# Hybrid decoder step on one core: meta tokens' values and weights in zero-filled tiles of their own, and the first tokens normalised in another order

## Chip, cores and metric

The kernel runs on one core of a Trainium2 chip. The metric is the device time of one execution in microseconds, as the median of several executions. Engines are called as the profile calls them: PE (matrix products), PEld (its weight loads), DVE, ACT, POOL and SP; a queue of an engine that issues transfers has a q behind its name (ACTq).

## The reference, cut to what matters

One layer over 16 learned meta tokens, 512 prompt tokens and 8 sample tokens, in float32. All tokens are normalised, and one projection gives the queries, keys and values of both groups of heads; eight heads are a linear recurrence (HGRN2), eight are differential attention. The weights of an attention head are the difference of two softmaxes, and keys 0 to 15 of every query are the meta tokens.

```python
def project(h, norm_g, w_in, lb):
    z = rmsnorm(h, norm_g) @ w_in
    hq, hf, hi, hg, aq, ak, av, ag = jnp.split(z, SPLIT_OFFSETS, axis=-1)
    ...

def diff_attend(q, k, v, q_pos, k_pos, rel_bias, lam):
    ...
    s = jnp.where(dist >= 0, s + bias, NEG_INF)
    p = jax.nn.softmax(s, axis=-1)
    w = p[:, 0] - lam * p[:, 1]
    return jnp.einsum('bhqk,bkhv->bqhv', w, v.astype(jnp.float32))
```

The sample tokens attend to 2048 cached keys each, which lie in pages, with a bias that is one value for all pages but the last and another for the last page.

## The kernel before, in words

All work stands in one program whose order on each engine is the order in which the Python code emits it; lines 1393 to 1399 bind it. Nearly every instruction is recorded through one helper, so the profile shows line 168 for it, and the tiles tell what it is.

The projection runs block by block (64 blocks of 128 columns for the inputs, 16 for the outputs). A block has four groups of 128x512 weights. `split` makes a high part (`hi`, on ACT) and a low part (`lo`, on DVE) of a group's weights, and `group` multiplies them on PE with the high and low parts of the tokens (`xh`, `xl`), 12 products for each half of the tokens. The first half is prompt tokens 0 to 255 (tiles 0 and 1), the second is tiles 2 and 3 with the meta and sample tokens.

Lines 439 to 483 are an order written out by hand, in which block 0 is multiplied while the prompt tokens are made. For tile j, `norm_stat(j)` takes squares with their sum and a reciprocal root on ACT (one chain of four instructions), `norm_scale(j, q)` scales a quarter on DVE, and `to_columns(j, g)` transposes a quarter on PE, copies it out of PSUM to `xh` on ACT and takes the difference to `xl` on DVE. Two halves of the PSUM space take the transposes in turn, two buffers each. Block 0 is multiplied in its halves by `group(u, xh, xl, z)`.

From then on the main loop issues one group after another, and after each of them lets a list of Python generators go on by one step: the attention of prompt heads (`attn`, four steps to a head, pipelined over steps n to n+4), the recurrence (`hgrn`), the softmax of sample tokens (`softmax_dec`), and products with cached values (`value_step`, PE, tile `t_pv`). A planner with its own clock (`fill`) decides where the DVE's work on cached keys stands.

For each value head, `attn_head` first calls `to_tok`: five transposes on PE into two PSUM buffers of the pool `tp` (which has two), the 24 meta and sample rows first; then two copies on ACT into one tile `vtok` (two buffers, shared with the head two before), and three stores on ACT's queue. In `attn`, a step transposes the weights of one 128-query block into `t_w` and those of the 16 meta keys into columns beside them, or, for the fourth block, into a buffer `t_w2` of its own, which the trace lists as t_w too. ACT copies them to `wT` and to `wmT` (16 rows). Every second step, the output `o` is the sum of products `vtok` by `wT`, and last of the product of the 16 meta rows, `vtok[0:NM, 4, :]` by `wmT`. So there are 16 meta products, two to a head: the first of a head adds to blocks 0 and 1, the second to blocks 2 and 3. The second one stands in the same step in which the tokens of a later head are transposed (lines 933 to 948).

Of the kernel before, what the change touches and what calls it, by code (L numbers as in the profile page):

```python
# [18 lines left out]
P = 128  # L19
# [3 lines left out]
NS = 8  # L23
# [186 lines left out]
def layer_kernel(ctx: ExitStack, tc: tile.TileContext, A):  # L210
# [40 lines left out]
    def tp(name):  # L251
        return clock.tile(pst.tile([P, 512], F32, name=name, tag="tp"), "tp", 2)
# [131 lines left out]
    def norm_scale(j, q):  # L384
        cs = slice(q * 512, (q + 1) * 512)
        V.scalar_tensor_tensor(xs[j][:, cs], xs[j][:, cs], stats[j], gB[:, cs], op0=ALU.mult, op1=ALU.mult)
# [51 lines left out]

    to_columns(0, 0)
    split(0)  # L440
    split(1)
    norm_scale(1, 1)
    to_columns(1, 0)
    to_columns(0, 1)
    norm_scale(1, 2)
    split(2)
    to_columns(1, 1)
    to_columns(0, 2)
    norm_scale(1, 3)
    norm_stat(2)  # L450
    to_columns(1, 2)
    to_columns(0, 3)
    to_columns(1, 3)
    group(0, xh, xl, 0)
    small_columns(0)
    small_columns(1)
    split(3)
    norm_scale(2, 0)
    norm_scale(2, 1)
    group(1, xh, xl, 0)  # L460
    norm_stat(3)
    small_columns(2)
    small_columns(3)
    to_columns(2, 0)
    norm_scale(2, 2)
    norm_scale(2, 3)
    to_columns(2, 1)
    group(2, xh, xl, 0)
    norm_scale(3, 0)
    to_columns(2, 2)  # L470
    norm_scale(3, 1)
    group(3, xh, xl, 0)
    to_columns(2, 3)
    norm_scale(3, 2)
    to_columns(3, 0)
    norm_scale(3, 3)
    to_columns(3, 1)
    group(0, xh, xl, 1)
    to_columns(3, 2)
    group(1, xh, xl, 1)  # L480
    to_columns(3, 3)
# [26 lines left out]
    lb = cp.tile([P, H], F32, name="lb")  # L508
    lb1 = cp.tile([P, H], F32, name="lb1")
    bm = cp.tile([P, 3, H], F32, name="bm")  # L510
    bdec = cp.tile([P, NPG, 2 * H], F32, name="bdec")
    b_far, b_near, b_new = bm[:, 0, :], bm[:, 1, :], bm[:, 2, :]
    rowd = dr.tile([H, W], F32, name="rowd")
    skew = dr.tile([H, P * W], F32, name="skew")
# [5 lines left out]
    def small_constants():  # L520
# [32 lines left out]
            T.matmul(t[:, i * H:(i + 1) * H], oh[:, OF + i * P:OF + (i + 1) * P], relb, start=True, stop=True)  # L553
        V.tensor_copy(bm.rearrange("p m h -> p (m h)"), t[:, :3 * H])
        for c in range(2):
            bv = bdec.rearrange("p g (h c) -> p g h c", c=2)[:, :, :, c]
            V.tensor_copy(bv[:, 0:NPG - 1, :], b_far.unsqueeze(1).to_broadcast([P, NPG - 1, H]))
            V.tensor_copy(bv[:, NPG - 1, :], b_near)
        for h in range(H):
            yield  # L560
            store(out=skew[h].rearrange("(p w) -> p w", w=W), in_=rowd[h:h + 1, :].to_broadcast([P, W]))
# [17 lines left out]
    gSa = cp.tile([P, H, NS], F32, name="gSa")  # L579
    amask = [cp.tile([P, P], F32, name=f"am{i}") for i in range(2)]  # L580
    ktail = [cp.tile([P, 2 * NM], F32, name=f"kt{i}") for i in range(2)]
    for a in amask + ktail:
        G.memset(a, 0.0)


# [211 lines left out]
    def softmax_dec(s):  # L797
        sco = scs[s]
        scp = sco[:, 0:NPG, :]
        V.tensor_tensor(scp, scp, bdec, op=ALU.add)  # L800
        V.tensor_copy(sco[:, NPG, :], snew[:, s].rearrange("p h c -> p (h c)"))
        mx = sm.tile([P, 2 * H], F32, name="mx", bufs=1)
        V.tensor_reduce(mx, sco.rearrange("p g a -> p a g"), axis=AX.X, op=ALU.max)
# [72 lines left out]
    def to_tok(src, h, name, tag, dst, dst_s):  # L876

        t2 = tp("t2_" + name)
        T.transpose(t2[:NM + NS, 0:P], src[:, NKEY:CT], ident)
        t = tp("t_" + name)  # L880
        for j in range(4):
            T.transpose(t[:, j * P:(j + 1) * P], src[:, NM + j * P:NM + (j + 1) * P], ident)
        tok = hw.tile([P, 5, P], F32, name=name, tag=tag, bufs=2)
        S.copy(tok[:NM + NS, 4, :], t2[:NM + NS, 0:P])
        S.copy(tok[:, 0:4, :].rearrange("p j d -> p (j d)"), t)
        store(out=dst[0, 0, NM:NKEY, h, :].rearrange("(j p) d -> p j d", p=P), in_=tok[:, 0:4, :])
        store(out=dst[0, 0, 0:NM, h, :], in_=tok[0:NM, 4, :])
        store(out=dst_s[0, :, 0, h, :], in_=tok[NM:NM + NS, 4, :])
        return tok

    def k_out(h):
        to_tok(ak[h], h, "ktok", "t5", A["k_prompt"], A["k_sample"])
# [20 lines left out]
    def attn_head(h):  # L913
        av = avs[h]
        strip = hw.tile([P, 528], F32, name="strip", tag="t1", bufs=2)
        flat = skew[h]
        clock.arrive(strip, 0.25)
        load(out=strip, in_=bass.AP(tensor=flat.tensor, offset=flat.offset, ap=[[W - 1, P], [1, 528]]))
        vtok = to_tok(av, h, "vtok", "t5", A["v_prompt"], A["v_sample"])
        G.tensor_copy(avS[:, :, h], av[:, T0:CT])  # L920
        for c in range(2):
            cs = slice(c * 64, (c + 1) * 64)
            G.tensor_copy(ktail[h % 2][cs, c * NM:(c + 1) * NM], ak[h][cs, SEQ:NKEY])
        heads[h] = dict(h=h, strip=strip, vtok=vtok, nm=sm.tile([P, 3, 4], F32, name="nm"),
                        s1=sm.tile([P, 4, 2], F32, name="s1"))
        flag(f"head{h}")
        yield
# [3 lines left out]
    def attn():  # L931
        live = {}
        for n in range(4 * H + 4):
            h, j = divmod(n, 4)
            if n < 4 * H and j == 0:
                if f"head{h}" not in flags or flags[f"head{h}"] >= slot[0]:
                    yield f"head{h}"
                head = heads[h]
            i4, i3, i2, i1 = (live.get(n - d) for d in (4, 3, 2, 1))
            if i4:  # L940
                a, jj = i4["head"], i4["j"]
                if jj % 2:
                    o = psv.tile([P, 512], F32, name="o", tag="pv")
                    for i in range(jj):
                        T.matmul(o[:, :2 * P], a["vtok"][:, i, :], a["wT"][:, (2 * i + 1) * P:(2 * i + 3) * P], start=i == 0, stop=False)
                    T.matmul(o[:, P:2 * P], a["vtok"][:, jj, :], a["wT"][:, 0:P], start=False, stop=False)
                    T.matmul(o[:, :2 * P], a["vtok"][0:NM, 4, :], a["wmT"], start=False, stop=True)
                    S.copy(aq[:, a["h"], (jj - 1) * P:(jj + 1) * P], o[:, :2 * P])
                if jj == 3:
                    flag(f"attn{a['h']}")  # L950
                    spawn(norm_chain(aq[:, a["h"], 0:SEQ], SEQ, gat, "ra"), f"attn{a['h']}")
                del live[n - 4]
            if i3:
                a, jj = i3["head"], i3["j"]

                L2, odd = (jj + 1) * P, jj % 2
                t = tp("t_w")
                for i in range(jj + 1):
                    x = NM + (i - odd) % (jj + 1) * P
                    T.transpose(t[:, i * P:(i + 1) * P], i3["p"][0][:, x:x + P], ident)  # L960
                t2, c2 = (t, L2) if jj < 3 else (tp("t_w2"), 0)
                T.transpose(t2[:NM, c2:c2 + P], i3["p"][0][:, 0:NM], ident)
                if not odd:
                    a["wT"] = hw.tile([P, 7 * P], F32, name="wT", tag="t4", bufs=1)
                    a["wmT"] = sm.tile([NM, 2 * P], F32, name="wmT", tag="wmT", bufs=1)
                w2 = a["wT"].rearrange("p (c q) -> p c q", q=P)
                S.copy(w2[:, 0:2 * jj + 1:2] if odd else w2[:, 1:2 * jj + 2:2], t[:, :L2].rearrange("p (c q) -> p c q", q=P))
                S.copy(a["wmT"][:, odd * P:(odd + 1) * P], t2[:NM, c2:c2 + P])
            if i1:
                a, L1 = i1["head"], (i1["j"] + 1) * P + NM  # L970
                for c in range(2):
# [47 lines left out]
    def hgrn(h):  # L1019
# [23 lines left out]
        vt = tp("t_hvt")  # L1043
        for j in range(4):
            T.transpose(vt[:, j * P:(j + 1) * P], v[:, NM + j * P:NM + (j + 1) * P], ident)
        hv8 = sm.tile([NS, P], F32, name="hv8", tag="wmT", bufs=1)
        S.copy(hv8, t[:NS, 0:P])
        store(out=hvd[h], in_=hv8)
        vkm = sm.tile([NM, 2, P], F32, name="vkm", bufs=1)
# [376 lines left out]
```

## Time and profile before

| | us |
|---|---|
| median of 3 executions | 1240.04 |
| lowest, highest | 1238.72, 1245.06 |
| profiled execution, device time | 1245.11 |
| span of the profiled execution, first to last instruction | 1243.3 |

Busy time and share are of the profiled execution. It is longer than the median, so the sum that is made on it is set against both. [...]

### The profile page before, as it was taken

The numbers are of one execution on the slowest core, as the hardware profiler recorded it, in microseconds if no ns is written. First come the engines' busy times: TensorE is split into PE (matmuls) and PEld (weight loads), VectorE is DVE, ScalarE is ACT, GpSimd is POOL, SyncE is SP. The second block draws the span as 40 slices with busy tenths as digits, with TensorE's granted clock in tenths as the row PEclk, the third lists the DMA queues.
The fourth block names the chain that finished last, engine by engine and source line by source line (L and its number), as shares of the span: only waits on it lengthen the run. The fifth ranks groups of instructions, "written<-read, shape, count | busy, mean of one in ns | idle before, by whom it ended". The sixth has DMA issues, their size and how long they took to land.

```text
span 1243.3 us, 24937 instructions
## 1 busy us (share of the span) xinstructions
PE 1207.9 (97%) x9352; PEld 1094.5 (88%) x9352; DVE 897.7 (72%) x1678; ACT 532.6 (43%) x1255; POOL 143.2 (12%) x151
## 2 busy tenths in 40 slices
PE   8999999999999999999999999999999999999995
PEld 6899999986677677888888889999999999999995
DVE  7522498878888888878897886989988956345253
ACT  6322333344545564445355465565422235323223
POOL 2000000100000000012010120122123310022020
PEclk9999999999999999999999999999999999999998
DMA  7353788836666669888888976757978837432223
GB/s 232 98 161 93 238 280 289 287 119 220 223 224 207 187 215 305 287 279 267 290 276 289 324 242 204 240 169 243 268 215 247 257 99 238 115 91 86 86 69 138
DMA packets 240958, 261.03 MB, mean 210 GB/s; under 512 B 8783, under 2 KB 198962, under 8 KB 240171
## 3 DMA queue, kind: packets, MB, share of 16 engines
q1 hardware_dynamic: 57298, 164.09, 38.3%
q10 hardware_dynamic: 183538, 95.34, 27.0%
q8 instruction: 74, 1.21, 0.4%
q14 instruction: 48, 0.39, 0.1%
HBM read 245.94 MB, written 16.14 MB: 211 GB/s over the span
## 4 chain that ended last, share of the span: by engine, by line
PE 79%; DVE 10%; DMA 4%; ACT 3%; issue 2%; ACTq 1%; SPq 0%; DVEq 0%
PE ps L168 65%; PE t_pv L168 4%; DVE qb L168 2%; DVE pgt L168 2%; DVE scd L168 2%; PE o L168 1%; PE ho L168 1%; DVE lo L168 1%; DMA raw<-in_w_out 1%; PE sc L168 1%; DMA raw<-in_w_in 1%; PE up L168 1%; PE t_w L168 1%; PE at L168 1%; DVE p L168 1%
## 5 line engine op out<-in xcount | busy, mean ns | idle before, releaser
L168 PE MATMUL ps<-xh,hi 128*128 128x264 f32 (+2 forms) x2048 | 539.8, 294 | 1.2 <-ACT ak L168 0.8
L168 PE MATMUL ps<-xl,hi 128*128 128x264 f32 (+2 forms) x2048 | 522.5, 286 | 1.1 <-DVE xl L168 1.1
L168 PEld LDWEIGHTS ps<-xh,hi 128*128 128x128 f32 x2048 | 387.5, 189 | 51.6 <-issue 41.7
L168 DVE TENSOR_TENSOR lo<-raw,hi 128x512 fp32r<-128x512 f32 x321 | 253.5, 795 | 216.5 <-ACT hi L168 215.6
L168 PEld LDWEIGHTS ps<-xl,hi 128*128 128x128 f32 x2048 | 388.0, 189 | 2.8 <-issue 2.7
L168 PE MATMUL ps<-xh,lo 128*128 128x264 f32 (+2 forms) x2048 | 333.1, 285 | 0.0
L168 ACT CAST hi<-raw 128x512 fp32r<-128x512 f32 x321 | 196.2, 617 | 242.9 <-PE ps L168 196.0
L168 PEld LDWEIGHTS ps<-xh,lo 128*128 128x128 f32 x2048 | 283.9, 189 | 0.0
L168 DVE TENSOR_TENSOR pgt<-pgt,qb 128x1024 f32<-128x1024 f32 x128 | 156.3, 1221 | 11.7 <-DMA pgt<-in_cache_k 7.0
L168 DVE TENSOR_REDUCE scd<-pgt 128x16 f32<-128x1024 f32 x128 | 155.6, 1216 | 1.7
L168 PE MATMUL ps<-mh,hi 128*128 128x256 f32 (+1 forms) x512 | 129.9, 286 | 0.2 <-ACT y L168 0.2
L168 PE MATMUL ps<-ml,hi 128*128 128x256 f32 (+1 forms) x512 | 128.5, 283 | 0.0
L168 DVE SCALAR_TENSOR_TENSOR qb<-pgt,wd,qb 128x128 f32<-128x128 f32 x360 | 106.8, 371 | 0.0
L168 PEld LDWEIGHTS ps<-mh,hi 128*128 128x128 f32 x512 | 96.5, 188 | 0.7 <-ACT y L168 0.4
L168 PEld LDWEIGHTS ps<-ml,hi 128*128 128x128 f32 x512 | 96.6, 189 | 0.0
L168 PE MATMUL ps<-mh,lo 128*128 128x256 f32 (+1 forms) x512 | 82.4, 283 | 0.0
L168 PEld LDWEIGHTS ps<-mh,lo 128*128 128x128 f32 x512 | 70.3, 189 | 0.0
L168 PE MATMUL t_pv<-pgt,wd 128*32 128x512 f32 x320 | 48.2, 648 | 8.5 <-ACT wmT L168 4.6
L168 POOL TENSOR_TENSOR sd<-sd,vb 128x1024 f32<-128x1024 f32 x8 | 19.4, 2430 | 174.5 <-ACT vb L168 174.5
L168 ACT COPY hgm<-ho 128x128 f32<-128x128 f32 x32 | 8.5, 265 | 70.0 <-PE ho L168 69.9
L168 ACT ACTIVATE p<-p,nm 128x144 f32<-128x144 f32 (+3 forms) x64 | 36.1, 565 | 2.0 <-DVE nm L168 2.0
L168 DVE TENSOR_TENSOR xr<-xr,t_y 128x512 f32<-128x512 f32 (+1 forms) x17 | 11.2, 657 | 31.2 <-PE t_y L168 31.2
(242 smaller groups left out, 1156.0 us busy)
## 6 DMA issues: line engine op xcount, KB each, us to landing
pgt<-in_cache_k SPq DMA_DIRECT2D x128, 512.0 KB
pgt<-in_cache_v SPq DMA_DIRECT2D x128, 512.0 KB
raw<-in_w_in ACTq DMA_DIRECT2D x125, 512.0 KB
raw<-in_w_out ACTq DMA_DIRECT2D x32, 512.0 KB
x<-in_x_prompt SPq DMA_DIRECT2D x4, 1024.0 KB
qb<-qd SPq DMA_DIRECT2D x8, 512.0 KB
sd<-in_state_hgrn SPq DMA_DIRECT2D x8, 512.0 KB
vb<-hvd SPq DMA_DIRECT2D x8, 512.0 KB
```

Of the source, the lines that this page charges most:

```text
L168: r = f(*a, **k)
```

## The change

The order of lines 439 to 481 is another: the squares of tiles 2 and 3 are earlier, the splits of the weights later, and the groups of block 0 stand earlier between the transposes. Then the meta rows get a tile of their own, `few` (one buffer, which `hgrn` uses for its 8 sample rows too); `vmeta` (two) and `wmeta` (one) are 128-row tiles that are zeroed once, and the meta rows are copied to their first 16 rows, so that the meta product has 128 rows. `t_w2` comes from the pool `psv` instead of `tp`. The bias of the cached keys is kept once instead of for each page, and is added in two instructions instead of one.

```diff
     to_columns(0, 0)
     split(0)
-    split(1)
     norm_scale(1, 1)
     to_columns(1, 0)
+    norm_stat(2)
     to_columns(0, 1)
     norm_scale(1, 2)
-    split(2)
+    split(1)
     to_columns(1, 1)
+    group(0, xh, xl, 0)
     to_columns(0, 2)
     norm_scale(1, 3)
-    norm_stat(2)
+    split(2)
+    norm_stat(3)
     to_columns(1, 2)
+    group(1, xh, xl, 0)
+    norm_scale(2, 0)
     to_columns(0, 3)
     to_columns(1, 3)
-    group(0, xh, xl, 0)
     small_columns(0)
     small_columns(1)
     split(3)
-    norm_scale(2, 0)
+    to_columns(2, 0)
+    group(2, xh, xl, 0)
     norm_scale(2, 1)
-    group(1, xh, xl, 0)
-    norm_stat(3)
+    norm_scale(3, 0)
     small_columns(2)
     small_columns(3)
-    to_columns(2, 0)
+    to_columns(2, 1)
     norm_scale(2, 2)
+    to_columns(3, 0)
+    group(3, xh, xl, 0)
+    norm_scale(3, 1)
     norm_scale(2, 3)
-    to_columns(2, 1)
-    group(2, xh, xl, 0)
-    norm_scale(3, 0)
     to_columns(2, 2)
-    norm_scale(3, 1)
-    group(3, xh, xl, 0)
+    to_columns(3, 1)
+    norm_scale(3, 2)
+    group(0, xh, xl, 1)
     to_columns(2, 3)
-    norm_scale(3, 2)
-    to_columns(3, 0)
     norm_scale(3, 3)
-    to_columns(3, 1)
-    group(0, xh, xl, 1)
     to_columns(3, 2)
     group(1, xh, xl, 1)
     to_columns(3, 3)
...
-    bdec = cp.tile([P, NPG, 2 * H], F32, name="bdec")
+    bdec = cp.tile([P, 2, 2 * H], F32, name="bdec")
...
-            bv = bdec.rearrange("p g (h c) -> p g h c", c=2)[:, :, :, c]
-            V.tensor_copy(bv[:, 0:NPG - 1, :], b_far.unsqueeze(1).to_broadcast([P, NPG - 1, H]))
-            V.tensor_copy(bv[:, NPG - 1, :], b_near)
+            V.tensor_copy(bdec.rearrange("p g (h c) -> p g h c", c=2)[:, :, :, c], bm[:, 0:2, :])
...
-    for a in amask + ktail:
+    vmeta = [cp.tile([P, P], F32, name=f"vm{i}") for i in range(2)]
+    wmeta = cp.tile([P, 2 * P], F32, name="wmeta")
+    for a in amask + ktail + vmeta + [wmeta]:
         G.memset(a, 0.0)
...
-        V.tensor_tensor(scp, scp, bdec, op=ALU.add)
+        V.tensor_tensor(sco[:, 0:NPG - 1, :], sco[:, 0:NPG - 1, :], bdec[:, 0, :].unsqueeze(1).to_broadcast([P, NPG - 1, 2 * H]), op=ALU.add)
+        V.tensor_tensor(sco[:, NPG - 1, :], sco[:, NPG - 1, :], bdec[:, 1, :], op=ALU.add)
...
-        tok = hw.tile([P, 5, P], F32, name=name, tag=tag, bufs=2)
-        S.copy(tok[:NM + NS, 4, :], t2[:NM + NS, 0:P])
-        S.copy(tok[:, 0:4, :].rearrange("p j d -> p (j d)"), t)
+        tok = hw.tile([P, 4, P], F32, name=name, tag=tag, bufs=2)
+        few = sm.tile([NM + NS, P], F32, name="few", tag="few", bufs=1)
+        S.copy(few, t2[:NM + NS, 0:P])
+        S.copy(tok.rearrange("p j d -> p (j d)"), t)
...
+                S.copy(vmeta[h % 2][0:NM, :], head["few"][0:NM, :])
...
-                    T.matmul(o[:, :2 * P], a["vtok"][0:NM, 4, :], a["wmT"], start=False, stop=True)
+                    T.matmul(o[:, :2 * P], vmeta[a["h"] % 2], wmeta, start=False, stop=True)
...
-                t2, c2 = (t, L2) if jj < 3 else (tp("t_w2"), 0)
+                t2, c2 = (t, L2) if jj < 3 else (psv.tile([P, 512], F32, name="t_w2", tag="pv"), 0)
...
-                    a["wmT"] = sm.tile([NM, 2 * P], F32, name="wmT", tag="wmT", bufs=1)
...
-                S.copy(a["wmT"][:, odd * P:(odd + 1) * P], t2[:NM, c2:c2 + P])
+                S.copy(wmeta[0:NM, odd * P:(odd + 1) * P], t2[:NM, c2:c2 + P])
...
-        hv8 = sm.tile([NS, P], F32, name="hv8", tag="wmT", bufs=1)
+        hv8 = sm.tile([NS, P], F32, name="few", tag="few", bufs=1)
```

## Rows read from the trace of the kernel before

**Rows 1.** Busy time by engine, from the page: us, share of the span, instructions.
```profile
PE 1207.9 (97%) x9352; PEld 1094.5 (88%) x9352; DVE 897.7 (72%) x1678; ACT 532.6 (43%) x1255; POOL 143.2 (12%) x151
```

**Rows 2.** List of waits of PE: us in total, times, longest us.
```profile
PE t_pv L168 <- ACT wmT L168: 4.6, 6, 0.9
PE t_w L168 <- ACT vtok L168: 2.1, 6, 0.3
PE t_sum L168 <- ACT wT L168: 1.1, 1, 1.1
```

**Rows 3.** Timeline of the first 42 us: start, length, engine, operation.
```profile
14.46 1.97 PE L168 MATMUL t_x<-ident,x 128*128 128x128 f32 x8 [1.34 <-DVE x L168]
20.21 1.92 ACT L168 ACTIVATE junk<-x 128x2048 bf16<-128x2048 f32 x1
22.69 1.54 ACT L168 CAST xh<-t_x 128x512 fp32r<-128x512 f32 x3
23.29 1.89 DVE L168 TENSOR_TENSOR xl<-t_x,xh 128x512 fp32r<-128x512 f32 x3 [1.18 <-ACT xh L168]
31.21 1.03 PE L168 MATMUL t_x<-ident,x 128*128 128x128 f32 x8
34.56 0.36 PE L168 MATMUL ps<-xl,hi 128*128 128x264 f32 x1 [1.14 <-DVE xl L168]
35.50 0.65 PE L168 MATMUL ps<-xh,lo 128*128 128x264 f32 x4
41.39 0.28 PE L168 MATMUL ps<-xh,hi 128*128 128x256 f32 x1
```

**Rows 4.** Timeline around meta products: weight loads of PEld, then products of PE.
```profile
279.51 0.19 PEld L168 LDWEIGHTS o<-wT,vtok 128*128 128x128 f32 x1
279.94 0.19 PEld L168 LDWEIGHTS o<-wT,vtok 128*128 128x128 f32 x1
279.29 1.68 PE L168 MATMUL o<-wT,vtok 128*128 128x256 f32 x8
267.78 0.69 PE L168 MATMUL o<-wmT,vtok 16*128 16x256 f32 x2
268.41 0.33 PE L168 MATMUL t_w<-ident,p 128*128 128x128 f32 x1
```

**Rows 5.** Timeline of one head's second meta product and what follows.
```profile
280.90 0.69 PE L168 MATMUL o<-wmT,vtok 16*128 16x256 f32 x2
281.63 0.73 ACT L168 COPY vtok<-t_vtok 24x128 f32<-24x128 f32 x2 [6.02 <-PE o L168]
281.94 0.44 PE L168 MATMUL t_w<-ident,p 128*128 128x128 f32 x2 [0.34 <-ACT vtok L168]
284.26 0.25 ACT L168 COPY wmT<-t_w 16x128 f32<-16x128 f32 x1
284.56 1.08 PE L168 MATMUL t_pv<-pgt,wd 128*32 128x512 f32 x4 [0.78 <-ACT wmT L168]
```

**Rows 6.** Table by stretch: us, busy of PE, PEld, DVE, ACT, POOL, PEclk, DMA share, GB/s.
```profile
284.32:287.72 3.40, 3.16 (x13) 1.50 (x14) 3.26 (x12) 1.93 (x7) 0.00 (x0) 0.50 1.02 312
311.60:315.00 3.40, 2.66 (x21) 1.72 (x21) 2.99 (x10) 2.74 (x9) 0.00 (x0) 1.00 0.82 243
```

**Rows 7.** Timeline: second meta products of the next heads.
```profile
308.83 0.48 PE L168 MATMUL o<-wmT,vtok 16*128 16x256 f32 x1
335.14 0.48 PE L168 MATMUL o<-wmT,vtok 16*128 16x256 f32 x1
```

**Rows 8.** Timeline of ACT around key heads; chain: start, us, what.
```profile
194.12 0.42 ACTq L888 DMA_DIRECT2D out_k_sample<-ktok  x1
204.51 0.25 ACT L168 COPY ktok<-t_ktok 24x128 f32<-24x128 f32 x1 [2.12 <-PE t_ktok L168]
134.51 13.46 DMA raw<-in_w_in
```

**Rows 9.** Groups of DVE by line: count, busy us, mean ns, idle before.
```profile
L168 DVE TENSOR_TENSOR wnew<-scd 128x8 f32<-128x8 f32 x8 | 1.3, 159 | 0.0
```

More of the change, by code (lines that the diff above doesn't have):

```diff
@@ L882, in to_tok @@
             T.transpose(t[:, j * P:(j + 1) * P], src[:, NM + j * P:NM + (j + 1) * P], ident)
-        tok = hw.tile([P, 5, P], F32, name=name, tag=tag, bufs=2)
-        S.copy(tok[:NM + NS, 4, :], t2[:NM + NS, 0:P])
-        S.copy(tok[:, 0:4, :].rearrange("p j d -> p (j d)"), t)
[L886 to L889, printed above, removed]
+        tok = hw.tile([P, 4, P], F32, name=name, tag=tag, bufs=2)
+        few = sm.tile([NM + NS, P], F32, name="few", tag="few", bufs=1)
+        S.copy(few, t2[:NM + NS, 0:P])
+        S.copy(tok.rearrange("p j d -> p (j d)"), t)
+        store(out=dst[0, 0, NM:NKEY, h, :].rearrange("(j p) d -> p j d", p=P), in_=tok)
+        store(out=dst[0, 0, 0:NM, h, :], in_=few[0:NM, :])
+        store(out=dst_s[0, :, 0, h, :], in_=few[NM:NM + NS, :])
+        return tok, few
     def k_out(h):
@@ L918, in attn_head @@
         load(out=strip, in_=bass.AP(tensor=flat.tensor, offset=flat.offset, ap=[[W - 1, P], [1, 528]]))
-        vtok = to_tok(av, h, "vtok", "t5", A["v_prompt"], A["v_sample"])
+        vtok, few = to_tok(av, h, "vtok", "t5", A["v_prompt"], A["v_sample"])
         G.tensor_copy(avS[:, :, h], av[:, T0:CT])
@@ L923, in attn_head @@
             G.tensor_copy(ktail[h % 2][cs, c * NM:(c + 1) * NM], ak[h][cs, SEQ:NKEY])
-        heads[h] = dict(h=h, strip=strip, vtok=vtok, nm=sm.tile([P, 3, 4], F32, name="nm"),
+        heads[h] = dict(h=h, strip=strip, vtok=vtok, few=few, nm=sm.tile([P, 3, 4], F32, name="nm"),
                         s1=sm.tile([P, 4, 2], F32, name="s1"))
```

## Prediction

> **What bounds the kernel now.** I read the busy times first: PE is busy for 97% of the span, and no other engine for more than 72% [rows 1]. So a microsecond counts where PE loses it, and elsewhere only if PE comes to wait. The list of PE's waits is short [rows 2]: what it names of attention sums to 7.8 us, all waits for copies on ACT. Then I read the timeline of the first 42 us, where PE is not yet the bound: the squares of a token tile take ACT 2.48 us (start 20.21, next copy 22.69), the differences on DVE wait 1.18 us for the copies behind them, and PE waits 1.14 us for such a difference before the second half of block 0. Block 1 begins at 41.39 [rows 3]. Last I read the attention steps: the meta products [rows 4], the step in which a head's second meta product stands [rows 5], the granted clock [rows 6] and the spacing of heads [rows 7].
>
> The sum is made on the profiled execution, device time 1245.1 (span 1243.3). The median of the runs is 1240.0, 5.1 less; the term of the clock says why, as I read it.
>
> **First part: the order of the first tokens.** Nothing is added or removed; it is a question of who waits. I laid the old order end to end over PE, ACT and DVE, each step behind the one before it on its engine and behind what it reads, with lengths from the rows: a copy to `xh` holds ACT 0.5 us (three in 1.54), a squares chain 2.48; a scaling or a difference holds DVE 0.6 to 0.7 (three differences in 1.89); four transposes hold PE 0.5, and twice that before about 21.5 us, where eight take 1.97 instead of 1.03. Four products take 0.65 with an end of 0.28, so they follow each other at 0.12, and the twelve of a group and half block hold PE 1.4 us, or 2.6 at half pace [rows 3]. The laid-out end of block 0 is 41.5, against 41.39 in the row; so the laying-out is good to some tenths. The new order laid out in the same way ends at 42.7: 1.2 us later. Why: the squares of tile 2 now stand on ACT directly behind the copy of tile 1's first quarter, at 16.1, and five transposed quarters queue behind them; the next copy goes out at 18.6, DVE dries up for 1.65 us, since the two splits that gave it work there have been moved behind. The first group on PE now comes at 18.0, where PE is at half pace, and holds the next transposes for 2.6 us (DVE dry 0.6). The squares of tile 3, at 22.7, dry it for 1.6 again. In the old order the two chains cost DVE 1.4 and 0.8. At the end the new order has more left to do on PE beside DVE's last differences, which doesn't make up for it. If PE went to full pace some 3 us sooner, which its busier queue may bring, the new order would end level with the old, or 0.4 ahead. Tile 2 must have landed by 16.1; its squares at 20.21 show no wait, so no row says how much sooner they can start, at worst 4 us of ACT. With the split behind them, a load of weights on ACT's queue goes out later too, but its weights are first read in block 1. Term: +1.2, bounds -0.4 and +4.
>
> **Second part: the meta product with 128 rows.** Passes of 128 rows and 256 columns follow each other at 0.215 us (weight loads at 279.51 and 279.94, two passes apart). The two passes of a 16-row product take 0.63 until the next instruction can go (267.78 to 268.41), 0.20 more than two of 0.215. It also begins late: six passes of 256 and two of 128 columns (0.109 each, by the transposes at 31.21) would take 1.51 from 279.29, and the product begins 1.61 after it [rows 4]. So PE loses 0.10 + 0.20 = 0.3 us at each of 16 products, and a product that uses all rows like its neighbours should lose none of it. At the eight first products of a head nothing waits behind: 8 x 0.29 = -2.3 us. [...] The loss that the rows show lies between the passes, and I go by them.
>
> Eight second products of a head: in six of them a copy into the token tile on ACT waits until `o` is done (idle 6.02 before it), and only then frees the buffer for PE's `t_w`, which waits 0.34; after three stores on ACT's queue the copy of `wmT` comes at 284.26, and `t_pv` waits 0.78 for it [rows 5]. In the new kernel the 24 rows go to `few`, which doesn't share the token tile's buffers: its copy is done early and `t_w` doesn't wait. The 512-column copy still waits for `o`, so the ACT queue behind it moves up only by what `o` gains (0.20) and by the copy that went ahead of it (0.73 for both, less some 0.6 for the larger): 0.33 us, and with `t_pv` behind that queue this is what PE gains, 6 x 0.33 = -2.0, bounds -3.8 (the 0.34 and the 0.3 in full) and 0. What remains late there is ACT's queue with its three stores. Two more heads have no tokens behind them: 2 x 0.29 = -0.6.
>
> `t_w2` in another pool: one wait of 1.1 us for `wT` hits a small product (`t_sum`) which took the buffer of `t_w` in turn after `t_w2` [rows 2]; without `t_w2` it takes the other: -1.1, bounds -1.1 and 0.
>
> **Clock.** Four stretches of 3.4 us between 284 and 424 us have a granted clock of 0.50, that is 1.2 GHz, such as that from 284.32; a like step of another head, at 311.60, kept 1.00 [rows 6]. Each follows a step as in [rows 5], in which PE did a 16-row product and small transposes, and waited. The price: from one head's second meta product to the next are 27.93 us with such a stretch (280.90 [rows 5] to 308.83) and 26.31 without (308.83 to 335.14) [rows 7], so 1.6, which is also half of the 3.16 that PE is busy in it [rows 6]. Since the new step has full rows in the place of the 16 and less waiting, I expect all four to go: -6.4, bounds -6.4 and 0. The runs of before lie between 1238.7 and 1245.1, 6.4 apart, as far as four such stretches, so I read the profiled execution as one with four and the median as one with none or one.
>
> **Small things.** Eight copies of 16 rows to `vmeta`, 0.25 each as for `wmT` [rows 5], stand on ACT at a step where PE waits for none of its copies: 0; with that cover gone 2. Eight more additions on DVE, at most 0.16 each as the small ones of `wnew` [rows 9], lie beside PE's work: 0, at most +1.3. The bias copies, the zeroing on POOL and the `psv` buffer, which was free a step before, are 0.
>
> **The sum.** 1245.1 + 1.2 - 2.3 - 2.0 - 0.6 - 1.1 - 6.4 = 1233.9. On the median, where I take the stretches at half clock as mostly not there, 1240.0 + 1.2 - 6.0 = 1235.2. I forecast between them, 1234.5. That is 0.45% below the median; about 0.5%, 6.2 us, is what a measurement of this kernel can tell from no change, so the edge, 1233.8, lies right beside it.
>
> **Rivals.** The half clock stays, or moves to other steps: the step keeps its wait behind ACT's queue, and the start shifts all steps against the stretches. Against it: the product is the largest of the weak work there. A run with four of them gives 1233.9 + 6.4 = 1240.3. Chance 0.12.
>
> Rows don't matter (the padding does nothing): the products stay at 0.63, only the waits go; 1245.1 + 1.2 - 6.4 - 1.1 and 6 x 0.13 less makes 1238.0. Against it the pace in [rows 4]. [...] Chance 0.08.
>
> The start gains instead: if the squares on ACT come where DVE has work, the dry 3.8 us that I count there aren't lost, and the start ends some 3 us before mine: 1231.5. For it: my laying-out hangs on when PE's clock rises and on tenths in the queues. Chance 0.22.
>
> Slower: `few` has one buffer where the token tile had two, so a head's copy waits until the stores of the head before have left. Between the last store of one key head and the copy of the next lie 10.39 us (194.12 to 204.51). One load on the same queue took 13.46 us [rows 8]; if stores did, ACT would stand 3 us at each of eight key heads and the splits and PE behind it: 1234.5 + 24 = 1258. It decides from a landing time of 10.4 us on; against it, in the old kernel that load is the only one of this length in the chain. Chance 0.07.
>
> **How the numbers follow.** Forecast 0.51, rivals 0.12, 0.08, 0.22, 0.07. Range 1230 to 1240.3: it takes in the sooner start, the products without gain and the bounds of the small terms and a run with the half clock, and leaves out the stalled copies and what lies beyond two bounds at once. Faster by over 0.5%: the start's case and not quite half of the forecast, 0.44; slower 0.07; within 0.5% the rest, 0.49.
>
> **What would show it.** Block 1 should begin near 42.6, with DVE idle before two differences behind squares. Two passes of the meta product should stand 0.215 apart, and `t_w` follow without a wait for ACT, while `t_pv` still waits for the copy of the weights. Heads should be 26 us apart or less, with no stretch at 0.50. A start that ends before 41, waits of ACT's copies into `few`, or half-clock stretches at other heads would each prove a step wrong.

## The result and the profile after

| | before | after |
|---|---|---|
| median, us | 1239.18 | 1227.51 |
| lowest, highest | 1238.07, 1245.06 | 1225.88, 1229.28 |
| executions | 6 | 6 |
| profiled execution, device time | 1245.11 | 1226.96 |
| its span | 1243.3 | 1225.1 |
| ratio after to before, 95% interval | | 0.990 [0.9886, 0.9914] |

The kernel became 11.7 us faster, twice what was forecast (5.5), and the time lies 2.5 us below the forecast's range. PE's busy time fell from 1207.9 [rows 1] to 1195.9.

The list of PE's waits after (us in total, times, longest), which answers to [rows 2]. `t_w` for `vtok` and `t_sum` for `wT` are gone; `t_pv` still waits for the copy of the meta weights in six steps, 4.4 us in all where it waited 4.6.

```profile
PE t_pv L168 <- ACT wmeta L168: 4.4, 6, 0.8
PE t_x L168 <- DVE x L168: 4.2, 5, 1.6
PE t_x L168 <- issue: 2.3, 1, 2.3
PE t_pv L168 <- DVE st L168: 0.6, 1, 0.6
PE t_vtok L168 <- ACT few L168: 0.3, 1, 0.3
```

The timeline of the start after, for [rows 3] (in brackets the idle time before an instruction, and what ended it). Both squares chains leave DVE waiting 1.51 us for a copy, PE stands idle for 2.27 us in front of the transposes at 27.33, and block 1 begins at 42.70 instead of 41.39.

```profile
16.22 1.91 ACT L168 ACTIVATE junk<-x 128x2048 bf16<-128x2048 f32 x1
18.00 0.56 PE L168 MATMUL ps<-xh,hi 128*128 128x256 f32 x1
19.29 0.69 DVE L168 TENSOR_TENSOR xl<-t_x,xh 128x512 fp32r<-128x512 f32 x1 [1.51 <-ACT xh L168]
...
25.88 0.69 DVE L168 TENSOR_TENSOR xl<-t_x,xh 128x512 fp32r<-128x512 f32 x1 [1.51 <-ACT xh L168]
27.33 0.63 PE L168 MATMUL t_x<-ident,x 128*128 128x128 f32 x4 [2.27 <-issue]
...
42.70 0.28 PE L168 MATMUL ps<-xh,hi 128*128 128x256 f32 x1
```

A first meta product after, for [rows 4]: the last product with `wT` before it, the load of its weights, itself, and what follows. The next instruction goes 0.43 us after it begins (268.75 to 269.18), where it took 0.63.

```profile
268.52 0.38 PE L168 MATMUL o<-wT,vtok 128*128 128x128 f32 x2
268.64 0.30 PEld L168 LDWEIGHTS o<-wmeta,vm 128*128 128x128 f32 x2
268.75 0.60 PE L168 MATMUL o<-wmeta,vm 128*128 128x256 f32 x2
269.18 0.60 PE L168 MATMUL t_w<-ident,p 128*128 128x128 f32 x4
```

A step with a second meta product after, for [rows 5], another head of the same pattern. The 512-column copy starts at 307.25, 0.2 us after the meta product *begins*; before, both copies started when that product had ended (281.63, with the product from 280.90 to 281.59 [rows 5]). The three stores on ACTq (1.3 us) stand, as before, ahead of the copies `aq`, `wT`, `wmeta`.

```profile
307.05 0.60 PE L168 MATMUL o<-wmeta,vm 128*128 128x256 f32 x2
307.25 0.59 ACT L168 COPY vtok<-t_vtok 128x512 f32<-128x512 f32 x1 [1.70 <-PE o L168]
307.49 0.38 PE L168 MATMUL t_w<-ident,p 128*128 128x128 f32 x2
307.87 0.42 ACTq L888 DMA_DIRECT2D out_v_prompt<-vtok  x1
308.33 0.51 ACTq L889 DMA_DIRECT2D out_v_prompt<-few  x1
308.89 0.34 ACTq L890 DMA_DIRECT2D out_v_sample<-few  x1
309.69 0.25 ACT L168 COPY wmeta<-t_w 16x128 f32<-16x128 f32 x1
309.99 1.06 PE L168 MATMUL t_pv<-pgt,wd 128*32 128x512 f32 x8 [0.73 <-ACT wmeta L168]
```

The stretch of [rows 6] after, in the same table: the granted clock stays at 1.00, and between 43 us and PE's last product no stretch at half clock is left. (PEclk is the granted clock of PE as a share of the full one. Here and below half clock is a granted clock of 0.50, and what comes after PE's last product is left out.)

```profile
284.32:287.72 3.40, 3.05 (x24) 2.21 (x25) 3.22 (x12) 2.24 (x8) 0.00 (x0) 1.00 0.99 295
```

Where the 18.2 us between the two spans lie, by the starts of the blocks' first products in the two traces. A second step is the step with a head's second meta product; it is measured from the first product of the group ahead of it to the first product of the group behind it.

| part | predicted | found |
|---|---|---|
| start of block 1 | +1.2 | +1.3 |
| eight first meta products (0.33 each) | -2.3 | -2.7 |
| six second steps (0.75 each where no clock fell) | -2.0 | -4.5 |
| two heads without tokens behind | -0.6 | -0.5 |
| `t_sum` (in block 24) | -1.1 | -1.2 |
| four stretches at half clock | -6.4 | -6.2 |
| blocks 27 to 32, other slots for `t_pv` | 0 | -4.6 |
| blocks 33 to 42, where part of that comes back | 0 | +2.1 |
| all other blocks | 0 | -1.8 |

The first five are found between the same products in both traces. The half clock is what is left of blocks 18 to 26 (227.5 us before, 212.35 after) when the four parts that lie there are taken off. The rows sum to 18.2 within rounding. Of the last row, 1.1 us lies in block 49, which is shorter by as much in the traces of all twelve experiments too, so it belongs to this one execution of the kernel before and not to the change.

The +2.1 is in part work that has moved. A step of `value_step` is eight `t_pv` products; block 27 has two such steps before and one after, and block 41 has none before and one after:

```profile
715.29 1.36 PE L168 MATMUL t_pv<-pgt,wd 128*32 128x512 f32 x8
```

So blocks 27 to 42 together gain 2.5 us (272.0 to 269.5), and not 4.6.

### The profile page after: what moved, and what is told of

It is laid out like the page before. It is cut to its first block, busy times and chain, and to the rows that moved or that the text cites. A ratio compares the mean times of both kernels' runs of the same rounds, so it can differ in the third digit from the quotient of the medians.

```text
span 1225.1 us, 24954 instructions
## 1 busy us (share of the span) xinstructions
PE 1195.9 (98%) x9352; PEld 1092.5 (89%) x9352; DVE 899.0 (73%) x1684; ACT 534.8 (44%) x1263; POOL 142.1 (12%) x154
## 4 chain that ended last, share of the span: by engine, by line
PE 85%; DVE 7%; ACT 3%; DMA 3%; issue 1%; ACTq 0%; SPq 0%; DVEq 0%
PE ps L168 70%; PE t_pv L168 4%; PE ho L168 2%; DVE qb L168 1%; DMA raw<-in_w_out 1%; PE o L168 1%; PE sc L168 1%; DVE scd L168 1%; DMA raw<-in_w_in 1%; PE up L168 1%; DVE pgt L168 1%; PE t_w L168 1%; DVE lo L168 1%; PE at L168 1%; ACT junk L168 1%
## 5 line engine op out<-in xcount | busy, mean ns | idle before, releaser
L168 DVE TENSOR_TENSOR lo<-raw,hi 128x512 fp32r<-128x512 f32 x321 | 256.6, 804 | 211.4 <-ACT hi L168 210.9
L168 PE MATMUL t_pv<-pgt,wd 128*32 128x512 f32 x320 | 45.4, 604 | 5.8 <-ACT wmeta L168 4.4
L168 DVE TENSOR_TENSOR xr<-xr,t_y 128x512 f32<-128x512 f32 (+1 forms) x17 | 11.2, 656 | 31.2 <-PE t_y L168 31.2
```

What stands on the lines that cost most here:

```text
L168: r = f(*a, **k)
```

## The experiments

Each kernel was timed beside runs of the kernel before on the same chip; their medians are 1240.6 (first four), 1242.3 (next four) and 1241.4 (last four), and 1239.2 for the changed kernel. So medians of different groups compare to 2 or 3 us, and where less matters the traces decide, of which there is one for each kernel. The 0.33, 0.77 and the like below are differences between the same products of a block in two traces.

**1. The start's order alone**, put into the kernel before (lines 439 to 483 as after).

```diff
-    split(1)
     norm_scale(1, 1)
     to_columns(1, 0)
+    norm_stat(2)
     to_columns(0, 1)
     norm_scale(1, 2)
-    split(2)
+    split(1)
     to_columns(1, 1)
+    group(0, xh, xl, 0)
...
```

> The kernel before with only the new order of the startup (lines 439 to 483); the meta tokens' weights and products stay as they were. Theory A (the new order costs the start what the records of the changed kernel show: block 1 begins at 42.70 us there and at 41.39 us before): the start gets 1.3 us longer and nothing else moves, so 1239.2 + 1.3 = 1240.5 us, and block 1 begins at 42.7 us. Theory B (the new order is what gives the gain, by another way than through the start: another clock or another placement of later work): 1236 us or less.

Median 1243.07, ratio 1.0017 [0.9998, 1.0036]: no gain, so B falls. The profiled execution begins block 1 at 42.52, as A says; 1.3 us can't be told from 0 by these times, which are spread from 1239.2 to 1249.8; the profiled execution alone has 13.7 us at half clock in three places, the longest (6.8 us) in block 27, where PE waits 2.8 us for `st`.

**2. The old order in the changed kernel**, the same edit the other way round.

```diff
+    split(1)
     norm_scale(1, 1)
     to_columns(1, 0)
-    norm_stat(2)
...
```

> The changed kernel with the old order of the startup put back; only the meta tokens' part of the change is left. Theory A (the start order costs 1.3 us and the meta tokens' part gives all of the gain): 1227.5 - 1.3 = 1226.2 us, block 1 begins at 41.4 us. Theory B (the start order carries part of the gain): 1228.5 us or more.

Median 1226.73, ratio 0.9894 [0.9876, 0.9911]: on A's side, though the 0.8 below the changed kernel is less than these medians can tell. Block 1 begins at 41.97, where A had 41.4. Over all profiled executions, block 1 begins at 42.0 on the mean of eight with the old order (41.39 to 42.60) and at 42.8 on the mean of four with the new one (42.52 to 43.10), a difference of 0.8. The meta tokens' part carries the whole gain.

**3 and 4. `t_w2` alone, with and without the planner's knowledge.**

```diff
-                t2, c2 = (t, L2) if jj < 3 else (tp("t_w2"), 0)
+                t2, c2 = (t, L2) if jj < 3 else (psv.tile([P, 512], F32, name="t_w2", tag="pv"), 0)
```

and in run 4

```diff
-                t2, c2 = (t, L2) if jj < 3 else (tp("t_w2"), 0)
+                t2, c2 = (t, L2) if jj < 3 else (clock.tile(psv.tile([P, 512], F32, name="t_w2", tag="pv"), "tp", 2), 0)
```

> The kernel before with one edit: the tile t_w2 is taken from the pool psv (tag pv), so that the planner's clock no longer counts it in the ring tp. The products stay 16 rows deep. Theory A (the planner, which now sees a free buffer in the ring, puts the second-map products t_pv of blocks 27 to 29 into other slots, and there they find their data ready): the t_sum wait goes (1.2 us) and blocks 27 to 29 take 4.1 us less: 1239.2 - 5.3 = 1234 us, with the placements of the changed kernel in these blocks. Theory B (only the wait for the bank in the last slots is worth anything): 1238 us.

> The same edit (t_w2 from the pool psv), but the tile is still reported to the planner's clock as one of the ring tp, so that the order of the instructions on TensorE is that of the kernel before. Theory A (the gain of 4.1 us in blocks 27 to 29 comes of the planner's other slots): these blocks take as long as before, and only the t_sum wait goes: 1238.0 us. Theory B (the gain comes of the freed bank itself, whatever the planner places): 1234 us.

Medians 1234.39, ratio 0.9951 [0.9938, 0.9965], and 1239.15, ratio 0.9989 [0.9975, 1.0003]: A in both. The wait of `t_sum` is gone in both, 1.2 us in either trace. But blocks 27 to 29 take 53.1 us before, 52.6 in run 4, and 48.3 in run 3 (49.0 in the changed kernel). Part of this comes back later: blocks 33 to 42 take 1.4 us more than before in run 3 and 0.1 in run 4, so that over blocks 27 to 42 run 3 is 3.0 us shorter than run 4. `tp(...)` does two things: it takes a buffer of the pool, and it tells the planner's clock that the ring has moved on by one. In run 3, as in the changed kernel, the planner reckons without `t_w2`, and puts the products with cached values (`t_pv`) into other slots. Timeline of PE in block 27, first of before, where `t_pv` stands behind `t_mx` in a slot in which DVE is late with the state `st`:

```profile
490.22 0.28 PE L168 MATMUL t_mx<-ident,mx 128*16 128x128 f32 x1
491.74 1.06 PE L168 MATMUL t_pv<-pgt,wd 128*32 128x512 f32 x8 [1.25 <-DVE st L168]
```

and of run 3, where it comes one slot later and waits for nothing:

```profile
484.96 0.28 PE L168 MATMUL t_mx<-ident,mx 128*16 128x128 f32 x1
...
489.45 1.07 PE L168 MATMUL t_pv<-pgt,wd 128*32 128x512 f32 x8
```

In the list of PE's waits from 470 to 526 us, run 4 has the line that before has too, and run 3 has none:

```profile
PE t_pv L168 <- DVE st L168: 1.8, 2, 1.2
```

**5. The tile `few` alone**, read by a 16-row product (and the bias once).

```diff
-        tok = hw.tile([P, 5, P], F32, name=name, tag=tag, bufs=2)
-        S.copy(tok[:NM + NS, 4, :], t2[:NM + NS, 0:P])
+        tok = hw.tile([P, 4, P], F32, name=name, tag=tag, bufs=2)
+        few = sm.tile([NM + NS, P], F32, name="few", tag="few", bufs=3)
+        S.copy(few, t2[:NM + NS, 0:P])
...
-                    T.matmul(o[:, :2 * P], a["vtok"][0:NM, 4, :], a["wmT"], start=False, stop=True)
+                    T.matmul(o[:, :2 * P], a["few"][0:NM, :], a["wmT"], start=False, stop=True)
```

> The kernel before with the bias once and the first transposed tokens in a tile of their own (few, three buffers, so that no store holds it up); the meta tokens' product reads few and stays 16 rows deep, t_w2 stays in the ring tp, the startup is the old one. Theory A (the second-product step gains because the 512-column copy into vtok no longer shares a tile with the meta product, and so starts after the last product with wT, 0.42 us earlier): six heads by 0.42 = 2.5 us less than the 1241.1 us that the kernel before took on the mean of 23 runs: 1238.6 us, and in the trace the copy into vtok starts before the meta product does. Theory B (the extra gain of that step comes of the padded product itself): the same time as before, and the copy starts after the meta product as before.

Median 1232.77, ratio 0.9932 [0.9915, 0.995]: A's mechanism, with a gain of 8 us where A had 2.5. Timeline of one second step, with the copy 0.11 us behind the *start* of the meta product:

```profile
306.62 0.69 PE L168 MATMUL o<-wmT,few 16*128 16x256 f32 x2
306.73 0.58 ACT L168 COPY vtok<-t_vtok 128x512 f32<-128x512 f32 x1 [1.70 <-PE o L168]
309.17 0.25 ACT L168 COPY wmT<-t_w 16x128 f32<-16x128 f32 x1
309.47 1.07 PE L168 MATMUL t_pv<-pgt,wd 128*32 128x512 f32 x8 [0.38 <-ACT wmT L168]
```

The copy starts 0.11 after the meta product does, where it started 0.73 after it (308.83 [rows 7] to 309.56), 0.62 sooner; and ACT has only the larger copy to do there, 0.58 instead of 0.73. Together that is 0.77. In the two heads where no clock fell before the step gains 0.77 and 0.81, as much as in the changed kernel (9.01 to 9.07 us in five heads, there 9.03 to 9.09, before 9.84) and with 16 rows; A had counted 0.42 of it. And the profiled execution has no half clock between 43 us and PE's end, though its products have 16 rows. That no theory had said.

**6. `few` with the padding**, without the other pool and with the old start: two edits to the changed kernel.

```diff
-                t2, c2 = (t, L2) if jj < 3 else (psv.tile([P, 512], F32, name="t_w2", tag="pv"), 0)
+                t2, c2 = (t, L2) if jj < 3 else (tp("t_w2"), 0)
```

> The changed kernel with the old order of the startup and with t_w2 back in the ring tp: the padded meta products and few with one buffer, but neither the planner's new placement nor the new start. Theory A (each padded product saves 0.33 us over the 16-row one, 8 first and 6 second steps and 2 late heads, on top of the 0.42 us of the earlier copy): 1241.1 - 2.5 - 14 x 0.33 - 0.6 = 1233.4 us, some 1 to 2 us less where the half-clock stretches go too; the first products 0.43 us long against 0.63 us. Theory B (the padding is worth nothing by itself and only the placement in blocks 27 to 29 is): 1238.6 us.

Median 1232.52, ratio 0.9911 [0.9887, 0.9935]: 0.9 below A, about what A left open for the half clock, but only 0.25 below run 5 by the median (two of its six executions took 1226.6 and 1227.4, the others 1232 to 1234). In the trace the eight first products gain 0.33 each, as A says; the second steps gain nothing over run 5, since `t_pv` there waits 0.83 on the mean for ACT's queue, 5.0 us in six, instead of 0.37, 2.2 in six. And what is gained is partly given back in block 27: PE comes sooner to the slot of run 4's wait, waits longer for `st`, and the clock falls behind it, so that block 27 takes 2.7 us more than before. The product in the timeline, and the table of the stretch:

```profile
480.27 1.49 PE L168 MATMUL t_pv<-pgt,wd 128*32 128x512 f32 x8 [2.33 <-DVE st L168]
...
481.00:484.40 3.40, 3.40 (x17) 2.71 (x13) 2.60 (x4) 0.00 (x0) 0.00 (x0) 0.50 0.83 268
```

**7. Late stores in the changed kernel**: `to_tok` keeps the three stores of a v head in a list, and the attention step issues them at its end (those of a k head at once, as before).

```diff
-        store(out=dst[0, 0, NM:NKEY, h, :].rearrange("(j p) d -> p j d", p=P), in_=tok)
+        held.append(dict(out=dst[0, 0, NM:NKEY, h, :].rearrange("(j p) d -> p j d", p=P), in_=tok))
...
                                           op0=ALU.add, op1=ALU.min, accum_out=a["nm"][:, c, j:j + 1])
+            release()
             yield
```

> The changed kernel, but the three stores of each head's v tokens are issued on ScalarE's queue at the end of the attention step that follows, instead of right behind the copies into few and vtok. Theory A (what TensorE still waits for in the second-product step, t_pv for wmeta 0.73 us in each of six heads, is ScalarE's issuing of the stores ahead of the copies aq, wT and wmeta): the waits go and the time is 1227.5 - 6 x 0.73 = 1223.1 us. Theory B (the wait is of the copies themselves, or moves to the probabilities that VectorE makes): 1226.5 us or more.

Median 1222.49, ratio 0.985 [0.9829, 0.987]: A. The copy to `wmeta` comes 1.03 us after that to `vtok` instead of 2.44, ahead of the stores, `t_pv` follows the products `se` without a wait, and the second steps take 8.3 us in five heads, where they took 9.03 to 9.09:

```profile
306.35 0.59 ACT L168 COPY vtok<-t_vtok 128x512 f32<-128x512 f32 x1 [1.70 <-PE o L168]
307.38 0.26 ACT L168 COPY wmeta<-t_w 16x128 f32<-16x128 f32 x1
307.57 0.39 ACTq L881 DMA_DIRECT2D out_v_prompt<-vtok  x1
308.29 1.06 PE L168 MATMUL t_pv<-pgt,wd 128*32 128x512 f32 x8
```

The profiled execution (1226.3 us) is one of two among the five that took 4 us more than the rest; its trace, with a mean granted clock of 0.994, has a stretch at half clock in the start, from 28.34.

**8. A third order of the startup** in the changed kernel, laid out over PE, ACT and DVE with the rows' durations as in the prediction. It begins and ends:

```diff
+    norm_scale(1, 2)
+    to_columns(0, 1)
+    to_columns(0, 0)
+    norm_scale(1, 1)
+    split(0)
+    norm_stat(2)
...
+    split(3)
+    to_columns(3, 3)
+    group(3, xh, xl, 0)
+    group(3, xh, xl, 1)
```

> The changed kernel with a third order of the startup, laid out by hand with the durations of the rows (squares 2.5 us, transposes 0.11 each, xh 0.59, xl 0.69, scaling 0.74, groups of 12 products 0.118 each) so that TensorE waits less for VectorE. Theory A (the start is bound by the order of these short steps alone): block 1 begins at 37.5 us instead of 42.7, and the time is 1227.5 - 5.2 = 1222.3 us. Theory B (the start is bound by when x arrives and by VectorE's total work, whatever the order): block 1 begins after 41 us, 1226 to 1228 us.

Median 1221.48, ratio 0.9834 [0.9816, 0.9851]: A. The profiled execution, the longest of five, has one stretch at half clock, from 589.59. Block 1 begins at 37.25:

```profile
37.25 0.28 PE L168 MATMUL ps<-xh,hi 128*128 128x256 f32 x1
```

**9. The padding alone**, with the shared token tile (and the bias once).

```diff
+    wmeta = cp.tile([P, 2 * P], F32, name="wmeta")
+    for a in amask + ktail + [wmeta]:
...
+        if name == "vtok":
+            G.memset(tok[:, 4, :], 0.0)
...
-                    T.matmul(o[:, :2 * P], a["vtok"][0:NM, 4, :], a["wmT"], start=False, stop=True)
+                    T.matmul(o[:, :2 * P], a["vtok"][:, 4, :], wmeta, start=False, stop=True)
```

> The kernel before with the padding alone: the meta weights in one zeroed tile of 128 rows, and the meta product over all 128 rows of the token tile's fifth block (GpSimd zeroes it first, ScalarE copies the 24 rows into it); the 24 rows still share the token tile with the 512 columns, there is no tile few, t_w2 stays in the ring tp, the startup is the old one. The bias is kept once, for space. Theory A (the second-product step gains by the tile of its own alone, and the half-clock stretches follow its wait, not the 16 rows): the first products gain 0.33 each, 2.6 us; the second steps at most 0.33 each, less 0.2 for the zeroing; half-clock stretches are still seen at these steps: 1241.3 (the mean of the runs of before) - 2.6 - 0.8 = 1237.9 us. Theory B (as forecast: full rows keep the clock up): no half-clock stretch at the second steps, some 3 us less: 1234.5 us or less.

Median 1237.96, ratio 0.9968 [0.9952, 0.9984]: on A's side. The first products gain their 0.33; the second steps take 9.94 to 10.06 us where no clock fell, against 9.84 before, so the 0.2 us of the shorter product is gone behind the zeroing. A had let these steps gain 0.8 in all, so that the median meets A's 1237.9 is partly luck. One step is still followed by a stretch at half clock, the last row:

```profile
333.85 0.20 POOL L168 MEMSET vtok<- 128x128 f32 x1 [7.97 <-PE o L168]
334.09 0.73 ACT L168 COPY vtok<-t_vtok 24x128 f32<-24x128 f32 x2 [4.88 <-POOL vtok L168]
334.40 0.44 PE L168 MATMUL t_w<-ident,p 128*128 128x128 f32 x2 [0.61 <-ACT vtok L168]
337.13 1.07 PE L168 MATMUL t_pv<-pgt,wd 128*32 128x512 f32 x8 [0.90 <-ACT wmeta L168]
...
389.10:392.50 3.40, 3.35 (x14) 1.69 (x15) 3.25 (x12) 1.74 (x5) 0.00 (x0) 0.51 1.00 303
```

**10. Late stores in the kernel before**, the edit of run 7 there.

```diff
-        store(out=dst[0, 0, 0:NM, h, :], in_=tok[0:NM, 4, :])
+        held.append(dict(out=dst[0, 0, 0:NM, h, :], in_=tok[0:NM, 4, :]))
...
+            release()
             yield
```

> The kernel before with one edit: the three stores of each head's v tokens are issued at the end of the attention step that follows, as in the earlier run with late stores. The products stay 16 rows deep and the 24 rows stay in the token tile. Theory A (the half clock follows the waits of TensorE in that step, whatever the rows): the wait of t_pv for wmT (0.78 us in each of six heads) goes, 4.7 us, and with it the half-clock stretches, some 3 us on the mean: 1241.3 - 7.7 = 1233.6 us. Theory B (the 16-row products are what lets the clock fall): the stretches stay, 1236.6 us.

Median 1233.69, ratio 0.9924 [0.9898, 0.9949]: A. Five of the second steps take 9.0 us, the first, which is the longest in every one of the kernels, 9.5 (11.2 before, with half clock), and none of them is followed by half clock, with 16-row products. But in the profiled execution, the longest of six, the clock falls elsewhere, in block 27, where PE waits 4.34 us:

```profile
483.33 1.08 PE L168 MATMUL t_pv<-pgt,wd 128*32 128x512 f32 x4 [4.34 <-DVE st L168]
...
482.50:489.30 6.80, 5.97 (x26) 4.30 (x27) 4.42 (x8) 0.00 (x0) 0.00 (x0) 0.50 0.64 202
```

**11. The changed kernel without the padding**: the product of run 5 in the changed kernel.

```diff
-                    T.matmul(o[:, :2 * P], vmeta[a["h"] % 2], wmeta, start=False, stop=True)
+                    T.matmul(o[:, :2 * P], a["few"][0:NM, :], a["wmT"], start=False, stop=True)
```

> The changed kernel with the padding taken out again: the meta product has 16 rows, from few (three buffers) and a 16-row tile of weights; everything else is as in the changed kernel. Theory A (the padding is worth what the eight first products and the two late heads show, 0.33 each, and nothing in the second-product steps, which end by ScalarE's queue): 1227.5 + 2.7 + 0.5 = 1230.7 us, second steps 9.05 us as with the padding, no half-clock stretch there. Theory B (the second steps gain by the padding too): 1232.7 us. Theory C (16-row products bring the half-clock stretches back): 1234 us or more.

Median 1231.13, ratio 0.9906 [0.9882, 0.9931]: by the median 3.6 above the changed kernel, which is A, by the ratio only 0.7. The trace decides for A: blocks 18 to 26 take 215.7 us against 212.35. The first products take 0.33 more each, five of the six second steps are within 0.15 of the changed kernel and one is 0.16 longer, the two heads without tokens 0.34 and 0.19 longer, and no stretch at half clock comes back. Around a first meta product the load of its weights now begins with the product, 0.20 us behind the last product with `wT`, where in the changed kernel it begins 0.11 us ahead of its product, beside the one before:

```profile
267.62 0.28 PE L168 MATMUL o<-wT,vtok 128*128 128x128 f32 x1
267.82 0.29 PEld L168 LDWEIGHTS o<-wmT,few 16*128 16x128 f32 x2
267.82 0.69 PE L168 MATMUL o<-wmT,few 16*128 16x256 f32 x2
268.45 0.66 PE L168 MATMUL t_w<-ident,p 128*128 128x128 f32 x4
```

**12. Late stores and the third order together**, the edits of runs 7 and 8 in the changed kernel.

```diff
+    norm_scale(1, 2)
+    to_columns(0, 1)
...
+            release()
             yield
```

> The changed kernel with both edits that helped: the late stores and the third order of the startup. Theory A (the two gains lie in different stretches and add): 1227.5 - 5.0 - 6.0 = 1216.5 us. Theory B (the earlier start shifts the steps against the loads, and part of it is lost to a new wait): 1219 us or more.

Median 1217.68, ratio 0.980 [0.9774, 0.9828], 9.8 below the changed kernel: 1.2 above A and 1.3 below B's bound, which these medians can't tell apart. It beats both kernels. In the trace both gains are there in full: block 1 begins at 36.55, 6.15 sooner than in the changed kernel, and blocks 18 to 26 take 207.7 us against 212.35. The other blocks take 1.3 more together, so part of B is seen. In the list of PE's waits there is a line that the changed kernel hasn't, of which run 7 alone has 1.0 already,

```profile
PE ho L168 <- DVE am L168: 1.8, 2, 0.9
```

## Why the prediction was wrong

**The start** was right for the two profiled executions: the laid-out end of block 0 was 42.7 and the trace has 42.70, with the waits of DVE behind both squares. The execution of before was an early one, though; by the mean starts under run 2 the price is 0.8. The rival in which the start gains is out.

**The first meta products** were right: 0.29 predicted, 0.33 found, and runs 9 and 11 show them by themselves. The length of the loads is not what differs: the two of a 16-row product take 0.29 us in run 11 and the two of a 128-row one 0.30 after, and yet the product with 16 rows costs 0.33 more. By the lines of run 11 and after, what differs is when the load begins: with 128 rows beside the product ahead, 0.11 us before its own (268.64 and 268.75), with 16 together with its own (both at 267.82). The rival that the padding does nothing is out with it.

**The second steps** are the step that failed, at one sentence: "The 512-column copy still waits for `o`". It waits for the last reader of the *old token tile*, and with the meta rows moved to `few` and `vmeta` that is the last product with `wT`, not the meta product. So the copy, and with it ACT's queue up to `wmeta`, moves up by what the meta product took as well, and each step gains 0.75 instead of 0.33. Run 5 shows that it is this and not the padding: there the step gains the same with 16 rows. I had followed the wait to the tile that the instruction names ([rows 5] say `<-PE o`) and not to which of the products of `o` still reads the buffer in the new code.

**`t_w2`** was right as a wait (-1.1, found -1.2) and is the second step that failed, as a list of effects. That the edit is "0" beyond the wait overlooked that `tp(...)` reports to the planner. Runs 3 and 4, which differ in this alone, put 4.2 us between their blocks 27 to 29 and 3.0 between their blocks 27 to 42 (4.8 between the medians). In the changed kernel it is 2.5 over blocks 27 to 42; part of the 4.6 found up to block 32 is a step of `t_pv` that now stands in block 41.

**The clock**: all four stretches went, as predicted, but the reason was half wrong. What the trace of before shows of the prediction's 1.2 GHz is a pace: at 0.50, from 286.82 to 287.50, products of 272 columns start 0.23 us apart, 1.2 columns per ns; at 1.00, from 313.67 to 314.43, they start 0.13 apart. Full rows were neither needed (runs 5, 10 and 11 have 16 rows and no such stretch at these steps in their profiled executions) nor enough (run 9). What the stretches have in common in the traces is a wait of PE shortly ahead of them, or under way: 0.34 and 0.7 to 0.9 us at the second steps of before and of runs 1, 3 and 4 (0.61 and 0.74 in run 9); 2.3 to 4.3 for `st` in block 27 of runs 1, 6 and 10; 1.54 for `st` in run 8; 2.79 in the start of run 7. A wait didn't always bring one: two of the six second steps of before kept the full clock, and so did run 5 behind 1.9 for `st` and the changed kernel behind 2.27 in its start. So the length of one wait does not decide, and what does is open.

How much of the gain is the clock differs with the execution of before. The record has the mean granted clock of every execution: 0.988 to 0.997 for the 51 timed beside the experiments, 0.995 to 0.997 for the six of the changed kernel. The 51 take 1241.6 us on the mean, and the 19 of them with 0.995 or more take 1239.6. So half clock costs the kernel before some 2 us on the mean (an estimate from these means), and the 6.2 of the table are those of one long execution.

**The stores of `few`**, the slower rival, did not show: PE's wait for `few` is 0.3 us in all, once.

On the median the prediction's sum was 1235.2. With 0.42 more for six second steps (2.5), 2.5 for the slots of `t_pv` and 0.4 each for the first products and the start it is 1229.4, against 1227.51. Of the 1.9 that are left, 0.9 is that the sum started from a median of three executions (1240.04), which over six is 1239.18; the rest is not assigned, and half clock in the executions of before may be part of it. The range did not reach low enough because both errors are on one side, and because I had widened each term, not asked which edits could reach the planner.

## What to carry to other kernels

When an edit moves an operand out of a shared tile, list again who reads the old tile last: what was queued on it may now start several instructions sooner (in run 5 by 0.62 us). When a planner orders the code, an edit that looks like one buffer is also an edit of the order; compare the two orders of instructions, or ask which of the planner's books the line writes. And where an engine's queue issues stores ahead of copies that the bound engine waits for, move the stores behind the copies: in run 7 that changed no arithmetic and gave 5 us. Last, sum a gain over all the blocks up to where the two orders meet again: what a stretch loses may be work that stands in a later one.

## What the runs showed of the hardware

The pace of PE at the start does not rise at a fixed moment. It is read from the products here: the PEclk of the tables is 1.00 from 14 to 28 us in before and in run 3, at either pace. In run 3, with the old order, products of 256 columns were still 0.41 us long and 0.21 apart up to 26.53, and 0.29 long from 26.95; in the trace of before they were down to 0.28 at 22.85. Over eight profiled executions with the old order the rise comes between 21.5 and 27.3 us, over four with the new one, whose first group stands at 18.0, between 21.5 and 23.5. The eight starts of block 1 with the old order (41.39 to 42.60) stand in the same order as the eight rises. That may explain the 1.2 us between executions of the old order, and why the new order cost less on the mean than in the two profiled executions of before and after. Two lines of run 3's timeline:

```profile
26.53 0.41 PE L168 MATMUL ps<-xl,hi 128*128 128x256 f32 x1
...
26.95 0.29 PE L168 MATMUL ps<-xl,hi 128*128 128x256 f32 x1
```

That a small edit's gain can be given back by the clock was new to me too. In runs 6 and 10 PE came to a slot where DVE set the time, waited longer there than before (2.33 and 4.34 us against 1.25), and had a granted clock of 0.50 for 3.4 and 6.8 us, in run 6 from 0.73 us after the end of the wait (481.00), in run 10 from 0.83 before it (482.50). In run 8 the clock was at 0.50 from 589.59, behind a wait of 1.54:

```profile
588.18 1.06 PE L168 MATMUL t_pv<-pgt,wd 128*32 128x512 f32 x8 [1.54 <-DVE st L168]
```

Run 10, which takes the wait for the weights out of the second steps and has no half clock there, speaks for the waits as the cause. The waits that brought none keep that open.
